# Attention scores: the second pass with 64 rows, two matmuls side by side in TensorE's array

## The chip, the cores and the metric

The kernel runs on one core of a Trainium2 chip. The core has a matrix engine (TensorE, in the profile PE for matmuls and PEld for its weight loads), three engines for everything else (VectorE, ScalarE and GpSimd: DVE, ACT, POOL) and a queue that issues most DMAs (SyncE, SP). The metric is the time of one execution in device microseconds (us); lower is better.

## The reference

One layer of a hybrid decoder, on 1024 tokens of width 1024 in float32. A projection feeds three mixers that run side by side; their outputs are normalised, mapped back by one output projection and added to the input; then comes an MLP. The mixer that matters here is the attention, with 8 query heads of 64 channels in 2 groups of 4 that share a key head. Its queries meet three sets of keys: compressed blocks, selected blocks, and a sliding window.

```python
s_c = jnp.einsum('bhgqd,bhnd->bhgqn', qb, kc) * scale        # compressed keys
...
s_s = jnp.einsum('bhgqd,bhqnld->bhgqnl', qb, k_sel) * scale  # selected blocks
...
s_w = jnp.einsum('bhgqd,bhkd->bhgqk', qb, kwb) * scale       # window of 512
...
o = gb[..., 0:1] * o_c + gb[..., 1:2] * o_s + gb[..., 2:3] * o_w
```

With 1024 tokens there are 16 blocks of 64 and 16 are selected, so the second branch sees all keys up to the query.

## The kernel before

The attention is worked through in sixteen units: one for each block of 128 queries (`i`) and each key head (`g`), four query heads (`h`) in a unit. A matmul here has 128 queries as its weights and runs the keys past them as columns; the scores of one head land in a tile of 1024 float32 in PSUM, two banks of 512.

The scores are computed with more accuracy than one pass of the fp32r format gives, by splitting both sides in a high and a low part. A channel dimension of 64 fills half of the array's 128 rows. The kernel therefore stacks the parts of the query: rows 0 to 63 of `qt` hold the high part and rows 64 to 127 the low part. The keys lie twice, once in each half of the rows: `kT[0]` holds their high part and `kT[1]` their low part. A matmul of `qt` with `kT[0]` gives high x high + low x high; a second one with `kT[1]` adds high x low + low x low.

`queries` makes `qt` for a unit: four transposes on TensorE, a copy of all 128 rows by ScalarE (L872), and a subtraction on rows 64 to 127 by VectorE (L873), which turns the copy there into the low part.

`scores` (L1034) serves one head whose keys are more than 512: it cuts the columns in two, one cut for each PSUM bank, and sends each cut through twice. `probs_few` (L1102) serves units with few keys, with two or four heads in one tile. Behind the scores `addmask` (L1042) and `mask` (L1108) add causal masks as matmuls of an identity in bf16. Then VectorE takes the maximum, ScalarE the exponential and GpSimd the scaling. `turn` (L1146) transposes the probabilities, and `values` (L1163, L1167) multiplies them with the values; the last piece of a unit's values, of the compressed branch, has 8 to 64 rows.

All these calls, with pieces of the output projection (`out_proj`, L896) as fillers, are sorted by due times that are written out by hand as fractions of a job, and are issued in that order; in the trace, pieces of neighbouring calls are at times interleaved on an engine. No due time is computed from an engine's cost.

Of the kernel before, what the change touches and what calls it, by code (L numbers as in the profile page):

```python
# [9 lines left out]
F32R = mybir.dt.float32r  # L10
BF16 = mybir.dt.bfloat16
I32 = mybir.dt.int32
AF = mybir.ActivationFunctionType
# [3 lines left out]
P = 128  # L17
# [5 lines left out]
DH = 64  # L23
# [13 lines left out]
def hymba_trunk(ctx: ExitStack, tc: tile.TileContext, ins: dict, out: bass.AP):  # L37
    nc = tc.nc
    act, dve, pool, pe = nc.scalar, nc.vector, nc.gpsimd, nc.tensor
# [11 lines left out]
    def f(ap):  # L51
        return ap.bitcast(F32)
# [19 lines left out]
    gq8 = cst.tile([P, 1], F32, name="gq8")  # L72
# [55 lines left out]
    def rpool(name):  # L128
        p_ = tc.tile_pool(name=name, bufs=1, side="right", reuse_waits="tile")
        right.append(p_)  # L130
        return p_.__enter__()
# [27 lines left out]
    with ExitStack() as pa:  # L159
# [554 lines left out]
        for s_, hf, b in proj_ch(C_KC, "kc"):  # L714
            o = hf * 512
# [34 lines left out]
        for qh in range(2):  # L750
            for t, b in proj_tok(C_Q + qh * 256, 256, f"q{qh}"):
# [4 lines left out]
                                  in_=sq.rearrange("p (a d) -> p a d", d=DH), axis=AX.X, op=ALU.add)  # L756
# [76 lines left out]
        kp2 = rpool("kp2")  # L833
        kwt = [[kp2.tile([P, S + 64], F32R, name=f"kwt{g}{j}") for j in range(2)] for g in range(2)]
        kst = [[kp2.tile([P, 64 + S], F32R, name=f"kst{g}{j}") for j in range(2)] for g in range(2)]
        qts = {}
# [23 lines left out]
        def queries(i, g, bank, qd):  # L860

            qd = qd.rearrange("p (h s d) -> p h s d", h=4, s=2)
            for s_ in range(2):
                pool.tensor_tensor(out=qd[:, :, s_, :],
                                   in0=qz[:, i, g * 256:(g + 1) * 256].rearrange("p (h d) -> p h d", d=DH),
                                   in1=rq[:, i * 8 + g * 4:i * 8 + g * 4 + 4][:, :, None].to_broadcast([P, 4, DH]), op=ALU.mult)
            yield
            b = bank(f"qT{i}{g}")
            for h in range(4):
                pe.transpose(b[:, h * P:(h + 1) * P], qd[:, h].rearrange("p s d -> p (s d)"), ident)  # L870
            qt = qts[i, g] = kp2.tile([P, 512], F32R, tag="qt", bufs=2, name=f"qt{i}{g}")
            act.activation(out=qt, in_=b, func=AF.Copy, scale=gq8)  # L872
            dve.scalar_tensor_tensor(out=qt[DH:P, :], in0=b[DH:P, :], scalar=gq8[DH:P, :], in1=f(qt[DH:P, :]),  # L873
                                     op0=ALU.mult, op1=ALU.subtract)

        lane(key_stack(1, 0, kdw, msbank))
        lane(queries(0, 0, msbank, spare[8]))
        for t in ks_:
            pass
# [119 lines left out]
    class Unit:  # L999
# [13 lines left out]
        def queries(self):  # L1013
            i, g = self.i, self.g
            if (i, g) not in qts:
                yield from queries(i, g, ring, spare[8])
            self.qt = qts.pop((i, g))
            self.nmx = uni.tile([P, 4, 3], F32, tag="nmx", bufs=2, name=f"nmx{i}{g}")
            self.sm = uni.tile([P, 4, 3], F32, tag="sm", bufs=2, name=f"sm{i}{g}")
            self.wt = uni.tile([P, 4, 3], F32, tag="wt", bufs=2, name=f"wt{i}{g}")  # L1020
            self.pc = uni.tile([P, 4, 64], F32, tag="pc", bufs=2, name=f"pc{i}{g}")

        def scores(self, h, kT, a, b_, name):

            n = b_ - a
            pt = psb.tile([P, 1024], F32, tag="s", bufs=2, name=name)
            if n <= 512:
                o, cuts = 0, [(0, n)]
            else:
                n0 = max(n - 512, min(512, n - 256))  # L1030
                o, cuts = 512 - n0, [(0, n0), (n0, n)]
            for (c0, c1) in cuts:
                for p_ in range(2):
                    pe.matmul(pt[:, o + c0:o + c1], self.qt[:, h * P:(h + 1) * P], kT[p_][:, a + c0:a + c1],  # L1034
                              start=p_ == 0, stop=False, skip_group_check=True)
            return pt, o

        @staticmethod
# [54 lines left out]
        def probs_few(self, br, h0):  # L1093

            i, g, m = self.i, self.g, self.few[br]
            kT, o, n = (kwt[g], 0, self.nw) if br == 2 else (kst[g], 64, self.nk)
            w, hs = 1024 // m, slice(h0, h0 + m)
            pt = psb.tile([P, 1024], F32, tag="s", bufs=2, name=f"sf{br}{i}{g}{h0}")
            by = pt.rearrange("p (h c) -> p h c", c=w)
            for j in range(m):  # L1100
                for p_ in range(2):
                    pe.matmul(pt[:, j * w:j * w + max(256, o + n)], self.qt[:, (h0 + j) * P:(h0 + j + 1) * P],  # L1102
                              kT[p_][:, 0:max(256, o + n)], start=p_ == 0 and j * w % 512 == 0, stop=False, skip_group_check=True)
            step_ = 512 // w

            def mask(c, mk, k):
                for j in range(0, m, step_):
                    pe.matmul(by[:, j:j + step_, c:c + k], identb, mk[:, None, :].to_broadcast([P, step_, k]),  # L1108
                              start=False, stop=True, skip_group_check=True)

            mask(o + n - P, m_causal, P)
            p_ = uni.tile([P, S], F32, tag="ps", bufs=PSB, name=f"pf{br}{i}{g}{h0}")
            parts = [(br, o, n, p_[:, 0:m * n].rearrange("p (h c) -> p h c", h=m))]
            if br == 1:
                mask(0 if i == 0 else 8 * i - 1, m_cmp[:, 1:9] if i == 0 else m_cmp, 8 if i == 0 else 9)
                parts.append((0, 0, self.ncm, self.pc[:, hs, :self.ncm]))
            for b_, c, k, dst in parts:
                dve.tensor_reduce(out=self.nmx[:, hs, b_], in_=by[:, 0:m, c:c + k], axis=AX.X, op=ALU.max, negate=True)
            for b_, c, k, dst in parts:
                for j in range(m):  # L1120
                    act.activation(out=dst[:, j, :], in_=by[:, j, c:c + k], func=AF.Exp, bias=self.nmx[:, h0 + j, b_:b_ + 1],
                                   accum_out=self.sm[:, h0 + j, b_:b_ + 1])
            for b_, c, k, dst in parts:
                wt = self.wt[:, hs, b_]
                gt = gates[:, i, :].rearrange("p (h b) -> p h b", b=3)[:, g * 4 + h0:g * 4 + h0 + m, b_]
                dve.reciprocal(wt, self.sm[:, hs, b_])
                dve.tensor_tensor(out=wt, in0=wt, in1=gt, op=ALU.mult)
                pool.tensor_tensor(out=dst, in0=dst, in1=wt[:, :, None].to_broadcast([P, m, k]), op=ALU.mult)
            for j in range(m):
                (self.pw if br == 2 else self.ps)[h0 + j] = parts[0][3][:, j, :]  # L1130
# [85 lines left out]
    for n, u in enumerate(units):  # L1216
# [5 lines left out]
        for part, br in ((0, 2), (1, 1)):  # L1222
# [3 lines left out]
            m = len(u.work[br])  # L1226
# [445 lines left out]
```

## Time and profile before

| | |
|---|---|
| median of three runs | 1255.13 us (1253.16 to 1256.38) |
| profiled execution, its own time | 1254.26 us |
| its span, first to last instruction | 1252.5 us |
| TensorE matmuls | 1205.0 us, 96% of the span, 6301 instructions |
| VectorE | 944.3 us, 75% |
| ScalarE | 675.8 us, 54% |
| GpSimd | 324.2 us, 26% |

A busy time is the union of an engine's instructions. Matmuls are pipelined, and the end of each is modelled, so that consecutive ones overlap on the page; the step from the start of one to the start of the next tells more than the duration. A form such as `64*128 64x512` means 64 rows and 128 columns of weights, and 512 columns that run past them.

### The profile page before, as it was taken

Reading aid. Unit: us, or ns where it says so; the run is one execution under the profiler, and the core shown is the slowest. Engines: PE = TensorE matmul, PEld = TensorE weight load, DVE = VectorE, ACT = ScalarE, POOL = GpSimd, SP = SyncE. Lnnn points to the kernel's source line nnn. Section 1 sums busy time; section 2 is a strip of 40 time slices with the busy share of each in tenths; the row PEclk is TensorE's granted clock in tenths of the full one; section 3 lists DMA queues with packets and bytes.
Section 4 is the critical chain, followed back from the end, with each engine's and each line's share of the span. In section 5 each row is a group of like instructions: output and inputs, shape, how many; then the busy total and the mean of one; then the engine's idle time right before and its main releaser. Section 6 shows DMA issues by size and latency. Waiting matters only on the chain.

```text
span 1252.5 us, 18215 instructions
## 1 busy us (share of the span) xinstructions
PE 1205.0 (96%) x6301; PEld 993.3 (79%) x6301; DVE 944.3 (75%) x1805; ACT 675.8 (54%) x1413; POOL 324.2 (26%) x347
## 2 busy tenths in 40 slices
PE   5999989979999999999799999999999999999998
PEld 5888878977777777777578888888878888888777
DVE  6899988658988989998867555555637897776684
ACT  6344367447677887776356545545544444444432
POOL 2357533335554456553760000000000000000000
PEclk9999999999999999999999999999999999999999
DMA  5322311212111200011424333333229933567640
GB/s 196 88 56 63 86 28 35 68 51 69 68 35 68 86 18 35 35 68 52 134 68 160 109 102 126 101 110 118 76 101 329 386 125 102 162 195 233 220 158 34
DMA packets 88584, 136.24 MB, mean 109 GB/s; under 512 B 8096, under 2 KB 42028, under 8 KB 88492
## 3 DMA queue, kind: packets, MB, share of 16 engines
q1 hardware_dynamic: 79276, 118.29, 29.2%
q10 hardware_dynamic: 9216, 16.78, 3.6%
q8 instruction: 50, 0.82, 0.3%
q14 instruction: 42, 0.34, 0.1%
HBM read 104.64 MB, written 29.36 MB: 107 GB/s over the span
## 4 chain that ended last, share of the span: by engine, by line
PE 81%; DVE 10%; ACT 3%; DMA 2%; POOL 2%; issue 1%; SPq 0%; ACTq 0%; DVEq 0%; POOLq 0%
PE y L1584 13%; PE z L1584 9%; PE t L1146 5%; PE rp L896 3%; PE op L896 3%; PE o L1163 3%; PE o L1167 3%; PE y L1387 2%; PE y L1389 2%; PE y L1388 2%; PE ss L1034 2%; DVE cv L515 2%; PE sw L1034 2%; PE kv L459 1%; PE kv L460 1%; PE kv L461 1%
## 5 line engine op out<-in xcount | busy, mean ns | idle before, releaser
L1149 ACT CAST ph<-t 128x512 fp32r<-128x512 f32 (+4 forms) x148 | 85.4, 585 | 44.6 <-PE t L1146 37.5
L1150 DVE TENSOR_TENSOR pl<-t,ph 128x512 fp32r<-128x512 f32 (+4 forms) x148 | 99.9, 683 | 6.1 <-ACT ph L1149 5.1
L1584 PE MATMUL y<-bl,ah 128*128 128x512 f32 x256 | 99.9, 390 | 1.8 <-DVE bl L1522 1.8
L1584 PE MATMUL y<-bh,al 128*128 128x512 f32 x256 | 99.6, 389 | 0.0
L1584 PE MATMUL y<-bh,ah 128*128 128x512 f32 x256 | 99.6, 389 | 0.0
L1304 ACT CAST whs<-s 128x512 fp32r<-128x512 f32 x64 | 39.9, 623 | 78.6 <-PE x L1388 32.1
L1584 PE MATMUL z<-bl,ah 128*128 128x512 f32 x192 | 75.0, 390 | 0.5 <-DVE bl L1522 0.5
L1584 PE MATMUL z<-bh,al 128*128 128x512 f32 x192 | 74.7, 389 | 0.0
L1584 PE MATMUL z<-bh,ah 128*128 128x512 f32 x192 | 74.7, 389 | 0.0
L1521 ACT CAST ah<-s 128x512 fp32r<-128x512 f32 x48 | 29.9, 623 | 75.7 <-PE y L1584 40.9
L214 POOL TENSOR_TENSOR wlo<-wst,whi 128x512 fp32r<-128x512 f32 (+1 forms) x36 | 52.6, 1474 | 61.8 <-ACT whi L213 61.5
L515 DVE SCALAR_TENSOR_TENSOR cv<-ypad,htap,cv 128x512 f32<-128x512 f32 x88 | 60.4, 752 | 0.4
L1305 DVE TENSOR_TENSOR wls<-s,whs 128x512 fp32r<-128x512 f32 x56 | 38.4, 685 | 26.6 <-ACT whs L1304 26.6
L1584 PEld LDWEIGHTS y<-bl,ah 128*128 128x128 f32 x256 | 48.1, 188 | 12.8 <-DVE bl L1522 2.8
L1584 PEld LDWEIGHTS y<-bh,ah 128*128 128x128 f32 x256 | 48.0, 188 | 10.0
L1584 PEld LDWEIGHTS y<-bh,al 128*128 128x128 f32 x256 | 48.0, 188 | 9.9
L1304 ACT CAST wha<-w 128x512 fp32r<-128x512 f32 x48 | 29.9, 622 | 39.1 <-PE y L1388 27.2
L1047 DVE TENSOR_REDUCE nmx<-ss 128x1 f32<-128x640 f32 (+8 forms) x72 | 43.5, 613 | 7.4 <-PE ss L1042 6.9
L1338 ACT ACTIVATE c<-c 128x512 f32<-128x512 f32 x48 | 30.4, 633 | 34.7 <-DVE c L1368 22.2
L1305 DVE TENSOR_TENSOR wla<-w,wha 128x512 fp32r<-128x512 f32 x42 | 28.9, 689 | 23.7 <-ACT wha L1304 23.6
L1521 ACT CAST ah<-x 128x512 fp32r<-128x512 f32 x32 | 19.9, 622 | 47.7 <-PE z L1584 34.2
L1522 DVE TENSOR_TENSOR al<-s,ah 128x512 fp32r<-128x512 f32 x48 | 33.2, 692 | 15.2 <-ACT ah L1521 14.8
(527 smaller groups left out, 3940.1 us busy)
## 6 DMA issues: line engine op xcount, KB each, us to landing
in<-in_mlp_w_dram SPq DMA_DIRECT2D x96, 256.0 KB
w<-in_mlp_w_dram SPq DMA_DIRECT2D x32, 512.0 KB
hid<-c ACTq DMA_DIRECT2D x48, 256.0 KB
in<-hid SPq DMA_DIRECT2D x48, 256.0 KB
wst<-in_w_in_dram SPq DMA_DIRECT2D x32, 256.0 KB
xr<-in_x_dram SPq DMA_DIRECT2D x8, 512.0 KB
x1p<-xr SPq DMA_DIRECT2D x8, 512.0 KB
x<-x1p SPq DMA_DIRECT2D x8, 512.0 KB
```

Of the source, the lines that this page charges most:

```text
L214: split[0] = pool.tensor_tensor(out=lo[:, :m], in0=st[:, :m], in1=f(hi[:, :m]), op=ALU.subtract).ins
L515: dve.scalar_tensor_tensor(out=acc[hf], in0=yp[:, o:o + 512], scalar=tap(k, ct), in1=acc[hf], op0=ALU.mult, op1=ALU.add)
L896: pe.matmul(b, a_[:, c * P:(c + 1) * P], w_, start=c == c0 and n == 0, stop=c == c1 - 1 and n == 2)
L1034: pe.matmul(pt[:, o + c0:o + c1], self.qt[:, h * P:(h + 1) * P], kT[p_][:, a + c0:a + c1], start=p_ == 0, stop=False, skip_group_check=True)
L1047: dve.tensor_reduce(out=nmx, in_=pt[:, c:c + n], axis=AX.X, op=ALU.max, negate=True)
L1146: pe.transpose(tb[:kn, h * P:(h + 1) * P], src(h), ident)
L1149: act.copy(ph[:kn], tb[:kn])
L1150: dve.tensor_tensor(out=pl[:kn], in0=tb[:kn], in1=f(ph[:kn]), op=ALU.subtract)
L1304: act.copy(k4(hi), v)
L1305: eng.tensor_tensor(out=k4(lo), in0=v, in1=f(k4(hi)), op=ALU.subtract)
L1521: act.copy(hi, v)
L1584: pe.matmul(banks2[BANK[m]][t], a_[:, ts], b_, start=q == 0 and n == 0 and m in FIRST, stop=q == NPAIR - 1 and n == 2, skip_group_check=True)
```

## The change

The second pass, with the low part of the keys, is done with the 64 rows of the query's high part alone; the product low x low is left out. `queries` makes a second tile `qx` that holds the high part in rows 64 to 127, beside `qt`, whose rows 0 to 63 hold it as before. ScalarE's one copy of 128 rows becomes two copies of 64 rows each. `scores` cuts its columns into halves, sends both through with `kT[0]` and full rows, and then issues two matmuls with `kT[1]`: the first cut on rows 0 to 63 with `qt`, the second on rows 64 to 127 with `qx`. They write different PSUM banks. `probs_few` does the same with pairs of heads. The number of matmuls is the same.

```diff
--- before.py
+++ after.py
@@ -868,9 +868,13 @@
             b = bank(f"qT{i}{g}")
             for h in range(4):
                 pe.transpose(b[:, h * P:(h + 1) * P], qd[:, h].rearrange("p s d -> p (s d)"), ident)
-            qt = qts[i, g] = kp2.tile([P, 512], F32R, tag="qt", bufs=2, name=f"qt{i}{g}")
-            act.activation(out=qt, in_=b, func=AF.Copy, scale=gq8)
-            dve.scalar_tensor_tensor(out=qt[DH:P, :], in0=b[DH:P, :], scalar=gq8[DH:P, :], in1=f(qt[DH:P, :]),
+            qt = kp2.tile([P, 512], F32R, tag="qt", bufs=2, name=f"qt{i}{g}")
+            qx = kp2.tile([P, 512], F32R, tag="qx", bufs=2, name=f"qx{i}{g}")
+            qts[i, g] = qt, qx
+
+            act.activation(out=qx[DH:P, :], in_=b[DH:P, :], func=AF.Copy, scale=gq8[DH:P, :])
+            act.activation(out=qt[0:DH, :], in_=b[0:DH, :], func=AF.Copy, scale=gq8[0:DH, :])
+            dve.scalar_tensor_tensor(out=qt[DH:P, :], in0=b[DH:P, :], scalar=gq8[DH:P, :], in1=f(qx[DH:P, :]),
                                      op0=ALU.mult, op1=ALU.subtract)
 
         lane(key_stack(1, 0, kdw, msbank))
@@ -1014,7 +1018,7 @@
             i, g = self.i, self.g
             if (i, g) not in qts:
                 yield from queries(i, g, ring, spare[8])
-            self.qt = qts.pop((i, g))
+            self.qt, self.qx = qts.pop((i, g))
             self.nmx = uni.tile([P, 4, 3], F32, tag="nmx", bufs=2, name=f"nmx{i}{g}")
             self.sm = uni.tile([P, 4, 3], F32, tag="sm", bufs=2, name=f"sm{i}{g}")
             self.wt = uni.tile([P, 4, 3], F32, tag="wt", bufs=2, name=f"wt{i}{g}")
@@ -1024,15 +1028,19 @@
 
             n = b_ - a
             pt = psb.tile([P, 1024], F32, tag="s", bufs=2, name=name)
+            hs = slice(h * P, (h + 1) * P)
             if n <= 512:
-                o, cuts = 0, [(0, n)]
-            else:
-                n0 = max(n - 512, min(512, n - 256))
-                o, cuts = 512 - n0, [(0, n0), (n0, n)]
+                o = 0
+                for p_ in range(2):
+                    pe.matmul(pt[:, 0:n], self.qt[:, hs], kT[p_][:, a:b_], start=p_ == 0, stop=False, skip_group_check=True)
+                return pt, o
+            n0 = max(n // 2, n - 512)
+            o, cuts = 512 - n0, [(0, n0), (n0, n)]
             for (c0, c1) in cuts:
-                for p_ in range(2):
-                    pe.matmul(pt[:, o + c0:o + c1], self.qt[:, h * P:(h + 1) * P], kT[p_][:, a + c0:a + c1],
-                              start=p_ == 0, stop=False, skip_group_check=True)
+                pe.matmul(pt[:, o + c0:o + c1], self.qt[:, hs], kT[0][:, a + c0:a + c1], start=True, stop=False, skip_group_check=True)
+
+            for (c0, c1), q_, rows in zip(cuts, (self.qt, self.qx), (slice(0, DH), slice(DH, P))):
+                pe.matmul(pt[:, o + c0:o + c1], q_[rows, hs], kT[1][rows, a + c0:a + c1], start=False, stop=False, skip_group_check=True)
             return pt, o
 
         @staticmethod
@@ -1097,10 +1105,15 @@
             w, hs = 1024 // m, slice(h0, h0 + m)
             pt = psb.tile([P, 1024], F32, tag="s", bufs=2, name=f"sf{br}{i}{g}{h0}")
             by = pt.rearrange("p (h c) -> p h c", c=w)
+            c1 = max(256, o + n)
             for j in range(m):
-                for p_ in range(2):
-                    pe.matmul(pt[:, j * w:j * w + max(256, o + n)], self.qt[:, (h0 + j) * P:(h0 + j + 1) * P],
-                              kT[p_][:, 0:max(256, o + n)], start=p_ == 0 and j * w % 512 == 0, stop=False, skip_group_check=True)
+                pe.matmul(pt[:, j * w:j * w + c1], self.qt[:, (h0 + j) * P:(h0 + j + 1) * P], kT[0][:, 0:c1],
+                          start=j * w % 512 == 0, stop=False, skip_group_check=True)
+
+            for j0 in range(m // 2):
+                for j, q_, rows in ((j0, self.qt, slice(0, DH)), (j0 + m // 2, self.qx, slice(DH, P))):
+                    pe.matmul(pt[:, j * w:j * w + c1], q_[rows, (h0 + j) * P:(h0 + j + 1) * P], kT[1][rows, 0:c1],
+                              start=False, stop=False, skip_group_check=True)
             step_ = 512 // w
 
             def mask(c, mk, k):
```

## Rows read from the trace of the kernel before

**Rows 1.** Stretches: us; busy (instructions) of PE, PEld, DVE, ACT, POOL; PEclk; DMA share; GB/s.
```profile
262.00:310.00 48.00, 39.52 (x261) 33.04 (x259) 36.15 (x79) 29.81 (x110) 20.17 (x24) 0.96 0.21 71
310.00:600.00 290.00, 287.69 (x1725) 224.31 (x1723) 258.00 (x581) 212.38 (x526) 145.09 (x181) 1.00 0.15 53
```

**Rows 2.** Chain that ended last, 310 to 600 us, shares by line.
```profile
by line: PE t L1146 20.3%; PE op L896 12.9%; PE o L1163 11.9%; PE rp L896 11.6%; PE o L1167 11.3%; PE ss L1034 9.7%; PE sw L1034 7.0%; PE sf L1102 3.4%; PE qT L870 1.7%; PE ss L1042 1.6%; PE sw L1042 1.6%; issue 1.2%; ACT ph L1149 1.0%; DVE
```

**Rows 3.** Waits, 262 to 310 us: engine, line, releaser; total, times, longest.
```profile
PE t L1146 <- DVE wt L1127: 4.9, 1, 4.9
```

**Rows 4.** Lines L1034, L1102: count, ns min/median/max, first and last start, forms.
```profile
L1034 PE MATMUL ss<-kst,qt x160: 276/369/501, 357.8 to 570.2; 128*128 128x512 f32 x64, 128*128 128x320 f32 x32, 128*128 128x448 f32 x32, 128*128 128x256 f32 x32
L1034 PE MATMUL sw<-kwt,qt x128: 277/312/471, 348.6 to 558.5; 128*128 128x256 f32 x64, 128*128 128x384 f32 x48, 128*128 128x448 f32 x16
...
L1102 PE MATMUL sf<-kwt,qt x64: 277/338/582, 270.0 to 462.4; 128*128 128x256 f32 x32, 128*128 128x384 f32 x16, 128*128 128x512 f32 x16
L1102 PE MATMUL sf<-kst,qt x48: 278/310/454, 271.1 to 345.4; 128*128 128x256 f32 x16, 128*128 128x320 f32 x16, 128*128 128x448 f32 x16
```

**Rows 5.** TensorE in order of time, two stretches: start, us, what, count.
```profile
500.59 0.75 PE L1034 MATMUL sw<-kwt,qt 128*128 128x384 f32 x4
501.18 0.23 PE L1042 MATMUL sw<-mwin,identb 128*128 128x128 bf16 x1
...
1100.12 0.39 PE L1584 MATMUL z<-bh,ah 128*128 128x512 f32 x1
...
1100.80 0.39 PE L1584 MATMUL y<-bh,ah 128*128 128x512 f32 x1
```

**Rows 6.** Lines L1163 and L1167: the matmuls on the compressed branch's values.
```profile
L1163 PE MATMUL o<-ph,vct x16: 489/497/502, 289.7 to 598.8; 8*128 8x512 f32 x2, 16*128 16x512 f32 x2, 24*128 24x512 f32 x2, 48*128 48x512 f32 x2
...
L1167 PE MATMUL o<-pl,vct x16: 383/394/448, 290.0 to 599.8; 8*64 8x512 f32 x2, 16*64 16x512 f32 x2, 24*64 24x512 f32 x2, 48*64 48x512 f32 x2
```

**Rows 7.** Around the 64-row matmuls, 598 to 600.6 us: TensorE, then one load.
```profile
598.24 0.40 PE L1167 MATMUL o<-pl,vst 128*64 128x512 f32 x1
598.47 0.40 PE L1163 MATMUL o<-ph,vst 128*128 128x512 f32 x1
598.80 0.50 PE L1163 MATMUL o<-ph,vct 64*128 64x512 f32 x1
599.22 0.44 PE L1167 MATMUL o<-pl,vst 128*64 128x512 f32 x1
599.50 0.40 PE L896 MATMUL op<-wo,ah 128*128 128x512 f32 x1
599.83 0.44 PE L1167 MATMUL o<-pl,vct 64*64 64x512 f32 x1
600.20 0.50 PE L896 MATMUL op<-wo,ah 128*128 128x512 f32 x1
...
598.79 0.18 PEld L1163 LDWEIGHTS o<-ph,vct 64*128 64x128 f32 x1 [0.37 <-issue]
```

**Rows 8.** Weight loads of two 16-row matmuls.
```profile
321.28 0.18 PEld L1163 LDWEIGHTS o<-ph,vct 16*128 16x128 f32 x1
321.39 0.13 PEld L1167 LDWEIGHTS o<-pl,vct 16*64 16x64 f32 x1
```

**Rows 9.** A mask between two 32-row matmuls, TensorE.
```profile
495.25 0.49 PE L1163 MATMUL o<-ph,vct 32*128 32x512 f32 x1
495.67 0.18 PE L1042 MATMUL ss<-mcmp,identb 128*128 128x9 bf16 x1
495.78 0.44 PE L1167 MATMUL o<-pl,vct 32*64 32x512 f32 x1
```

**Rows 10.** Query copies L872, L873; idle of TensorE ahead of L1102.
```profile
L872 ACT ACTIVATE qt<-qT,gq x16: 663/690/740, 258.5 to 539.9; 128x512 fp32r<-128x512 f32 x16
...
L873 DVE SCALAR_TENSOR_TENSOR qt<-qT,gq,qt x16: 756/757/760, 259.4 to 540.8; 64x512 fp32r<-64x512 f32 x16
...
  DVE qt L873: 4.5, 5
```

## The prediction

> **What bounds the kernel now.** I read the stretches first. From 262 to 600 us, the attention over the sixteen units, the stage from 310 on keeps TensorE busy for 287.7 of 290 us at the full granted clock (1.00, the 2.4 GHz level), while VectorE has 258.0, ScalarE 212.4 and GpSimd 145.1 [rows 1]. A busy TensorE may still be a badly modelled one, so the second view is the chain that ended last, from 310 to 600: eleven TensorE lines lead it with 93% together, and the score lines are among them (L1034 ss 9.7%, sw 7.0%, L1102 3.4%) [rows 2]. So here a TensorE microsecond is a microsecond of the end, nearly one for one. Before 310, 8.5 of 48 us are idle [rows 1], 4.9 of them one wait for the first unit's weights [rows 3]; that unit's scores lie ahead of this wait, so their time counts too. VectorE, next in line, has 32 us of room from 310 on.
>
> The third view is the list of score instructions. L1034 has 160 + 128 matmuls, four for a call: 72 calls. L1102 has 64 + 48, which are 6 calls with four heads (eight matmuls of 256) and 16 with two heads: 22 calls [rows 4]. Every one is 128x128 with full rows. Half of each sum is the second pass: 53,760 columns in L1034, 13,312 in the two-head calls, 6,144 in the four-head calls.
>
> **What a matmul costs.** The printed duration holds a tail that overlaps the next one; the step from start to start is what counts. At 512 columns four matmuls in a row start from 1100.12 to 1100.80, three steps of 0.227 us [rows 5]. The four score matmuls of 384, 384, 256, 256 columns from 500.59 to the mask at 501.18 take 0.59 [rows 5]. Two equations: 0.016 us + 0.41 ns a column. Weight loads do not appear in it: they run under the matmul ahead.
>
> **What the change removes.** With the two halves fully side by side, half of the second-pass columns and one of two starts go: L1034 26,880 columns x 0.41 ns + 72 x 0.016 = 12.2 us; two-head calls 6,656 columns and 16 starts = 3.0; four-head calls 3,072 columns and 12 starts = 1.4. Sum 16.6 us. The first pass has the same columns in other cuts (all at least 288 wide): nothing.
>
> **What it adds on TensorE.** The number of matmuls stays, but between the first pass and the mask stand matmuls with 64 rows. The trace has 64-row and smaller ones already: the values of the compressed branch, 16 on L1163 and 16 on L1167 [rows 6]. Around them the steps are longer. The clearest stretch is the last [rows 7], all of 512 columns, where 0.23 is normal:
> - 128 rows at 598.47 to 64 rows at 598.80: 0.33. The weight load of the 64-row one starts only at 598.79, so it waited until the array had finished: **0.10 to drain**.
> - 64 rows at 598.80 to 128 rows at 599.22: 0.42. It is 0.21 of columns, another 0.10 to drain, and 0.11 that the 64-row weight load takes in the open.
> - 599.50 to 599.83, into 64 rows once more: 0.33, the same 0.10.
> - 598.24 to 598.47, from 64 columns to 128 with all rows: 0.23, nothing. It is the change of rows that costs.
>
> A 32-row one behaves alike: 0.42 from 495.25 to 495.67 [rows 9]. So for each of the 94 calls:
> 1. Draining ahead of the pair: 0.10.
> 2. The first 64-row load in the open: 0.11 [rows 7].
> 3. The second load. No row shows weights for the upper 64 rows. The nearest: among small-row matmuls a load may run under a matmul, but two loads follow each other by 0.11 (321.28, 321.39) [rows 8]. If so, the second matmul starts 0.11 behind the first and the pair ends 0.11 late. Bounds: 0, if both loads run at once, to 0.11; I take 0.11.
> 4. Draining behind the pair: 0.10.
> 5. The mask's weights in the open. A nine-column mask just after a 32-row matmul steps 0.11 to the next, which changes rows again [rows 9]: 0.10 of it drains, so the bf16 load is about 0.02.
>
> Together 0.44 us a call, 41.4 for 94. In the four-head calls four loads follow each other, 0.44 from the first, and the last matmul ends 0.10 later than steps 2 and 3 allow: 6 x 0.1 = 0.6. Sum 42.0, net **42.0 - 16.6 = +25.4 us**. A call with 640 columns, say: second pass before 0.29, after 0.44 + 0.15 = 0.59.
>
> The Trainium skill ("TensorEngine Tiling (Array Packing)", Key Properties) says that a change of tiling mode drains the array and a change of tile alone does not. Rows 7 show the first half; no row here shows the second. By that rule nothing drains between the two matmuls of a pair, as my sum has it.
>
> **What it adds elsewhere.** The copy L872 (0.69 us, 16 times) becomes two copies of 64 partitions. No row shows a copy of 64 partitions; the subtraction L873 works on 64 and takes 0.757 [rows 10], so I take the full 0.69 for each half: at most 16 x 0.69 = 11 us more on ScalarE, which has 77 us of room from 310 on [rows 1]. VectorE waits only for the first of the two, and works 0.76 while ScalarE does the other, so the query is ready no later. TensorE waited 4.5 us in all for a query [rows 10]; what queues behind the new copy on ScalarE is the next cast of L1149, 0.69 later. TensorE grows slower than its suppliers, so I price this at 0; with the cover gone it would be 0.69 for a late query, 11 at the very most. The masks, VectorE's and GpSimd's instructions and the DMAs stay. Four KB more a partition for the second query tile lie in space whose earlier users, the projections, are ahead of the transposes on TensorE anyway: 0.
>
> **What is given back.** Waits of TensorE that other engines end get shorter when TensorE comes later: of the 8.5 + 2.3 us idle [rows 1] most is the 4.9 behind the first unit's own scores; I take 2 back (bounds 0 and 4). So 1254.26 + 25.4 - 2 = 1277.7. The profiled run lies 0.9 below the median 1255.13; I say **1277.5**.
>
> **Rivals.**
> - *Both loads at once* (step 3 is 0): 94 x 0.33 = 31.0, less 16.6 = +14.4, less 2: 1266.7. Against it, the 0.11 between two loads [rows 8]; for it, those were for the same rows. The skill ("TensorE: Matmul & The Clock Gate", Part 3) says that loads run beside matmuls when their row groups differ and that packed tiles start about 4 ns apart; if that holds with both loads still to do, this rival is the outcome. Chance 0.13.
> - *The halves do not overlap*: the second load then hides under the first matmul and the second pass keeps its columns; 94 x 0.33 = +31, less 2: 1283.3. No row shows two matmuls in the array at once. The gap to my forecast is small, because the late second load eats most of the overlap. Chance 0.15.
> - *Each matmul of a pair drains, too*: no overlap, and 0.21 more a pair (steps 1 and 2 again): 100 pairs x 0.21 = 21 on top of the last one: 1304. Chance 0.05.
> - *The rows change without a stop*, the one on the other side: the work side by side, 16.6 us gone, 1237.7 (VectorE's 258.0 of then 273 us would still fit). For it, the free change of columns [rows 7]; against it all the 32 small-row matmuls. It decides once entering and leaving cost less than 16.6 / 94 = 0.18 us a call, where I count 0.44. Chance 0.08.
> - *No change to be seen*: the call costs about what it saves, 0.14 to 0.24 with the 2 us given back; step 3 gone and the draining half as long would do it: 94 x 0.23 - 16.6 - 2 = +3, 1257. Chance 0.04.
>
> **How the numbers follow.** My forecast has 0.55. The two slower neighbours and the quick loads keep to one side, and with them 0.83 lies from 1264 (quick loads, 4 us given back: 1264.7) to 1289 (no overlap, nothing given back, and a few pairs torn apart by a transpose that TensorE runs in between, at some 0.3 each). Three runs of before lie within 0.26%, so 0.3%, 3.8 us, is what can be told from no change. Slower by more: 0.55 + 0.13 + 0.15 + 0.05 = 0.88; within: 0.04; faster: 0.08.
>
> **What would show it.** In the profile after, the weight load of the first 64-row matmul starts when the matmul ahead has ended, 0.10 late; the second load 0.11 behind it; the start of the pair's second matmul within 0.15 of the first, not a whole matmul later; the second pass with what surrounds it 0.59 us at 640 columns, in place of 0.29. The attention stage grows by some 23 us and all behind it moves as a block. VectorE's and ScalarE's idle time grows. The prediction is wrong if the 64-row load runs under the first pass, if a TensorE wait for the query tiles grows to some us, or if the granted clock leaves 1.00 in this stage.

## The result

The changed kernel takes 1274.58 us in the median of five runs (1271.64 to 1279.25), against 1255.13 before: a ratio of 1.0151, 95% interval 1.0137 to 1.0165. It is 19 us slower. 1277.5 was forecast, with a range of 1264 to 1289. Its profiled execution is the slowest of the five, 1279.25 us with a span of 1277.2. Of the runs below, one execution of switch_twice took 3171 us and one of copy_pool 5746 us; the ratios leave these two out, the medians count them.

### The profile page after: what moved, and what is told of

Same layout as the page of the kernel before. It is cut to its first block, busy times and chain, and to the rows that moved or that the text cites. A ratio compares the mean times of both kernels' runs of the same rounds, so it can differ in the third digit from the quotient of the medians.

```text
span 1277.2 us, 18230 instructions
## 1 busy us (share of the span) xinstructions
PE 1224.7 (96%) x6301; PEld 983.6 (77%) x6301; DVE 949.7 (74%) x1805; ACT 687.8 (54%) x1429; POOL 324.4 (25%) x347
## 4 chain that ended last, share of the span: by engine, by line
PE 80%; DVE 10%; ACT 4%; POOL 3%; DMA 2%; issue 1%; SPq 0%; ACTq 0%; POOLq 0%; DVEq 0%
PE y L1597 13%; PE z L1597 9%; PE t L1159 4%; PE rp L900 3%; PE op L900 3%; PE o L1176 2%; PE o L1180 2%; PE y L1400 2%; PE y L1402 2%; PE y L1401 2%; DVE cv L515 2%; PE kv L459 1%; PE kv L460 1%; PE kv L461 1%; PE y L1342 1%
## 5 line engine op out<-in xcount | busy, mean ns | idle before, releaser
L1163 DVE TENSOR_TENSOR pl<-t,ph 128x512 fp32r<-128x512 f32 (+4 forms) x148 | 99.6, 683 | 5.6 <-ACT ph L1162 4.3
L214 POOL TENSOR_TENSOR wlo<-wst,whi 128x512 fp32r<-128x512 f32 (+1 forms) x36 | 50.9, 1426 | 61.5 <-ACT whi L213 61.1
L1597 PEld LDWEIGHTS y<-bl,ah 128*128 128x128 f32 x256 | 48.3, 189 | 12.5 <-DVE bl L1535 2.3
L1055 DVE TENSOR_REDUCE nmx<-ss 128x1 f32<-128x768 f32 (+8 forms) x72 | 43.7, 617 | 11.0 <-PE ss L1050 10.5
```

What stands on the lines that cost most here:

```text
L214: split[0] = pool.tensor_tensor(out=lo[:, :m], in0=st[:, :m], in1=f(hi[:, :m]), op=ALU.subtract).ins
L1055: dve.tensor_reduce(out=nmx, in_=pt[:, c:c + n], axis=AX.X, op=ALU.max, negate=True)
L1163: dve.tensor_tensor(out=pl[:kn], in0=tb[:kn], in1=f(ph[:kn]), op=ALU.subtract)
L1597: pe.matmul(banks2[BANK[m]][t], a_[:, ts], b_, start=q == 0 and n == 0 and m in FIRST, stop=q == NPAIR - 1 and n == 2, skip_group_check=True)
```

## The profile after

The page's first part, and the granted clock in 40 slices of the span:

```profile
PE 1224.7 (96%) x6301; PEld 983.6 (77%) x6301; DVE 949.7 (74%) x1805; ACT 687.8 (54%) x1429; POOL 324.4 (25%) x347
...
PEclk9999989988999999999989999999999999999999
```

The number of matmuls is the same. ScalarE has 16 instructions and 12 us more.

Two stretches of the attention, with the columns of [rows 1]:

```profile
262.00:310.00 48.00, 39.17 (x243) 30.91 (x242) 34.64 (x75) 29.22 (x106) 19.35 (x24) 0.93 0.20 67
310.00:600.00 290.00, 283.40 (x1631) 197.70 (x1630) 246.70 (x535) 213.57 (x524) 144.27 (x179) 0.98 0.13 46
```

From 310 on TensorE is busy for 283.4 of 290 us, where it was 287.7 [rows 1]: it waits more than before. The granted clock is 0.98 in this stretch, where it was 1.00: for 10.2 us from 311 on it is at half, the 1.2 GHz level. The same 10.3 us in the profile after and in the one before:

```profile
311.00:321.30 10.30, 9.79 (x37) 6.96 (x35) 6.52 (x13) 6.53 (x22) 2.68 (x3) 0.51 0.17 53
311.00:321.30 10.30, 10.30 (x61) 8.36 (x59) 9.50 (x24) 6.81 (x23) 6.94 (x10) 1.00 0.00 1
```

That costs about half of the 10.2 us, 5 us (an estimate). The last score matmul starts at 593.3, where it was 570.2 [rows 4]; this is the line of the second pass, upper rows:

```profile
L1043 PE MATMUL ss<-kst,qx x40: 393/449/502, 370.1 to 593.3; 64*128 64x416 f32 x8, 64*128 64x352 f32 x8, 64*128 64x288 f32 x8, 64*128 64x480 f32 x8
```

The chain that ended last, 310 to 622 us:

```profile
by line: PE t L1159 17.8%; PE op L900 11.8%; PE rp L900 11.0%; PE o L1176 9.7%; PE o L1180 9.3%; PE ss L1040 4.4%; PE ss L1043 4.3%; PE sw L1040 3.5%; PE sw L1043 3.3%; PE sf L1115 2.3%; PE sf L1110 2.3%; PE ss L1050 2.3%; PE sw L1050 2.2%;
```

It is still TensorE's, and the second pass (L1043, L1115) has its own share in it, 10% with ss, sw and sf together.

One call of 640 columns in order of time, matmuls first and then weight loads:

```profile
520.64 0.46 PE L1040 MATMUL sw<-kwt,qt 128*128 128x320 f32 x2
521.02 0.41 PE L1043 MATMUL sw<-kwt,qt 64*128 64x320 f32 x1
521.03 0.41 PE L1043 MATMUL sw<-kwt,qx 64*128 64x320 f32 x1
521.37 0.23 PE L1050 MATMUL sw<-mwin,identb 128*128 128x128 bf16 x1
521.44 0.22 PE L1050 MATMUL sw<-mcausal,identb 128*128 128x128 bf16 x1
...
521.02 0.18 PEld L1043 LDWEIGHTS sw<-kwt,qt 64*128 64x128 f32 x1 [0.19 <-issue]
521.03 0.18 PEld L1043 LDWEIGHTS sw<-kwt,qx 64*128 64x128 f32 x1
521.37 0.11 PEld L1050 LDWEIGHTS <-identb 128*128 128x128 bf16 x2 [0.16 <-issue]
```

The two first passes start at 520.64, 0.15 apart, and the pair at 521.02: 0.09 after the second of them should have ended. The first 64-row load starts there too, with TensorE's loads idle for 0.19 before it. **The second load and the second matmul start within 0.01 us of the first**, and not 0.11 behind. From the pair to the mask it is 0.35 us: 0.11 for the loads, 0.13 for 320 columns, 0.10 to drain. The whole second pass takes 0.44, where 0.59 was forecast and it took 0.29 before. So each call is 0.15 longer; over 94 calls, 94 x 0.30 of entering and leaving less the 16.6 us saved are about 12 us. To check this I added up, over every score matmul of the trace, the time from its start to the start of TensorE's next matmul: 73.8 us before, 86.5 after. That is 12.7 of 19 us; some 1.5 of the 12.7 come from the clock (an estimate: 4.9 us of these steps lie at half clock, where it was 1.9, and half of the difference is lost). The rest had to be looked for.

## The experiments

All ratios are against the kernel before, run on the same chip.

| run | median us | ratio | 95% interval |
|---|---|---|---|
| low_rows | 1287.08 | 1.0250 | 1.0235 to 1.0265 |
| full_rows | 1265.78 | 1.0079 | 1.0064 to 1.0094 |
| switch_twice | 1314.58 | 1.0467 | 1.0449 to 1.0484 |
| two_heads | 1275.13 | 1.0160 | 1.0138 to 1.0183 |
| cuts_only | 1256.38 | 1.0000 | 0.9992 to 1.0009 |
| copies_only | 1264.24 | 1.0066 | 1.0049 to 1.0082 |
| copy_pool | 1272.36 | 1.0116 | 1.0098 to 1.0133 |
| after_again | 1276.99 | 1.0147 | 1.0127 to 1.0166 |
| copies_late | 1260.20 | 1.0030 | 1.0019 to 1.0042 |
| copy_late | 1268.63 | 1.0099 | 1.0086 to 1.0112 |
| two_heads_tight | 1270.37 | 1.0113 | 1.0098 to 1.0127 |
| no_copy | 1264.33 | 1.0070 | 1.0058 to 1.0083 |

**Do the two halves overlap? (low_rows)** The upper matmul of each pair moves to the lower rows. It computes the same values.

```diff
-            for (c0, c1), q_, rows in zip(cuts, (self.qt, self.qx), (slice(0, DH), slice(DH, P))):
+            for (c0, c1), q_, rows in zip(cuts, (self.qt, self.qt), (slice(0, DH), slice(0, DH))):
...
-                for j, q_, rows in ((j0, self.qt, slice(0, DH)), (j0 + m // 2, self.qx, slice(DH, P))):
+                for j, q_, rows in ((j0, self.qt, slice(0, DH)), (j0 + m // 2, self.qt, slice(0, DH))):
```

> Both second-pass matmuls of a pair use rows 0 to 63, so they cannot lie side by side; the number of changes of rows stays. If the two halves do overlap in the changed kernel, each pair here is longer by one matmul of half the columns: 12.2 + 3.0 + 1.4 = 16.6 us in all, so about 16 us over the changed kernel (1291). Rival, that the 3 ns between their starts is only how the profile shows them and they run one after the other: no change against the changed kernel (1275).

Measured 1287.1, 12.5 us over the changed kernel's median. TensorE in order of time, one call of 640 columns again:

```profile
530.00 0.53 PE L1040 MATMUL sw<-kwt,qt 128*128 128x320 f32 x2
530.46 0.56 PE L1043 MATMUL sw<-kwt,qt 64*128 64x320 f32 x2
530.95 0.23 PE L1050 MATMUL sw<-mwin,identb 128*128 128x128 bf16 x1
```

From the pair to the mask it is now 0.49 us, where the changed kernel has 0.35. The difference, 0.14, is one matmul of 320 columns (0.15 by the prediction's price). The overlap is real. All score steps together sum to 101.1 us, 14.6 over the changed kernel, where 16.6 was expected; some 1.4 of the missing 2.0 are the changed kernel's own half clock (2.1 us of these steps lie there in low_rows, against 4.9). 12.5 show in the time.

**Is it the changes of rows? (full_rows, switch_twice)** The first keeps all of the change but runs the second pass on all 128 rows. The second changes rows twice in each of the 72 calls of `scores`.

```diff
# full_rows
+            for (c0, c1), q_, rows in zip(cuts, (self.qt, self.qt), (slice(0, P), slice(0, P))):
...
+                for j, q_, rows in ((j0, self.qt, slice(0, P)), (j0 + m // 2, self.qt, slice(0, P))):
# switch_twice
-            for (c0, c1) in cuts:
-                pe.matmul(pt[:, o + c0:o + c1], self.qt[:, hs], kT[0][:, a + c0:a + c1], start=True, ...)
             for (c0, c1), q_, rows in zip(cuts, (self.qt, self.qx), (slice(0, DH), slice(DH, P))):
+                pe.matmul(pt[:, o + c0:o + c1], self.qt[:, hs], kT[0][:, a + c0:a + c1], start=True, ...)
                 pe.matmul(pt[:, o + c0:o + c1], q_[rows, hs], kT[1][rows, a + c0:a + c1], start=False, ...)
```

> The changed kernel with its new cuts, its second query tile and ScalarE's extra copies, but with the second pass on all 128 rows again, so TensorE never changes rows for the scores. If the changes of rows are the cause, this is the kernel before: 1255, within 2 us. Rival, that the copies, the tile or the order of work that comes with them cost the 5 to 6 us by which the time lies over what the score matmuls alone add: 1260.

> In the 72 calls of the longer rows the order is first pass of cut 0, second pass of cut 0, first pass of cut 1, second pass of cut 1, so TensorE enters and leaves the 64-row form twice a call. If each change of rows has its price (0.10 to drain, 0.11 for a 128-column load in the open), a call has 0.42 us more and loses its overlap (12.2 us in all): 72 x 0.42 + 12.2 = 42 us over the changed kernel, 1317. Rival, that the price belongs to a 64-row matmul whatever stands beside it: only the overlap is lost, 1287.

The doubled changes cost what their price says: 1314.6, 40 us over the changed kernel, where 42 was expected and the rival had 12. But full_rows missed its main expectation. Without any change of rows it is still 10 us slower than the kernel before. So the rows account for only about half of the loss, and the change has a second cost, which the prediction put at nothing.

**Which part is the second cost? (cuts_only, copies_only)** cuts_only is full_rows with `queries` and its one tile as before. copies_only is the kernel before with the new `queries`:

```diff
-            qt = qts[i, g] = kp2.tile([P, 512], F32R, tag="qt", bufs=2, name=f"qt{i}{g}")
-            act.activation(out=qt, in_=b, func=AF.Copy, scale=gq8)
+            qt = kp2.tile([P, 512], F32R, tag="qt", bufs=2, name=f"qt{i}{g}")
+            qx = kp2.tile([P, 512], F32R, tag="qx", bufs=2, name=f"qx{i}{g}")
+            qts[i, g] = qt, qx
+            act.activation(out=qx[DH:P, :], in_=b[DH:P, :], func=AF.Copy, scale=gq8[DH:P, :])
+            act.activation(out=qt[0:DH, :], in_=b[0:DH, :], func=AF.Copy, scale=gq8[0:DH, :])
...
```

> The kernel before with the new cuts and the new order (both first passes, then both second passes) alone: one query tile, one copy of 128 rows, all matmuls on 128 rows. If ScalarE's copies and the second query tile are what made the full-row version 10 us slower, this is the kernel before: 1255, within 2 us. Rival, that the cuts and the order cost it: 1265.

> The kernel before with the second query tile and ScalarE's two 64-row copies alone; the scores are as before. If the copies cost the 10 us: 1265. Rival, that the cuts and the order do: 1255. If each has a part, both lie between.

The cuts and the order of the passes cost nothing (1.0000). The copies cost 8.3 us by themselves (1.0066). In copies_only TensorE is busy for 281.8 of 290 us, where the kernel before has 287.7:

```profile
310.00:600.00 290.00, 281.83 (x1679) 218.52 (x1678) 253.50 (x559) 218.07 (x533) 144.76 (x180) 0.99 0.14 49
```

**Where the copies hurt.** The last unit's query after: transposes on TensorE, ScalarE, then VectorE.

```profile
560.75 0.49 PE L870 MATMUL qT<-ident,spare 128*128 128x128 f32 x3
...
561.50 0.68 ACT L875 ACTIVATE qx<-qT,gq 64x512 fp32r<-64x512 f32 x1
562.21 1.12 ACT L1056 ACTIVATE ps<-ss,nmx 128x1024 f32<-128x1024 f32 x1
...
563.31 0.67 ACT L876 ACTIVATE qt<-qT,gq 64x512 fp32r<-64x512 f32 x1
...
564.10 1.43 DVE L988 SCALAR_TENSOR_TENSOR yf<-x,rm,gmn 128x512 f32<-128x512 f32 x2
...
565.69 0.76 DVE L877 SCALAR_TENSOR_TENSOR qt<-qT,gq,qx 64x512 fp32r<-64x512 f32 x1
```

And the same query before:

```profile
539.13 0.63 PE L870 MATMUL qT<-ident,spare 128*128 128x128 f32 x4
...
539.90 0.67 ACT L872 ACTIVATE qt<-qT,gq 128x512 fp32r<-128x512 f32 x1
...
540.83 0.76 DVE L873 SCALAR_TENSOR_TENSOR qt<-qT,gq,qt 64x512 fp32r<-64x512 f32 x1
```

Before, one copy follows the transposes, and VectorE ends its subtraction at 541.59. After, ScalarE does the first copy at 561.50, then an exponential of 1.1 us, then the second copy until 563.98; VectorE begins only at 565.69, since other work of its own (L988) stands ahead. The transposes end at 539.76 before and at 561.24 after (start and duration of their rows), so the way to the end of the subtraction has grown from 1.8 to 5.2 us. In the two units where VectorE stood idle ahead of the subtraction, it waited for the second copy:

```profile
L877 DVE SCALAR_TENSOR_TENSOR qt<-qT,gq,qx x16: 756/757/758, 261.5 to 565.7; 64x512 fp32r<-64x512 f32 x16
...
  ACT qt L876: 1.0, 2
```

In all 16 units the subtraction starts after the end of the second copy, by 0.03 to 1.7 us, though it reads only the first. That both write the tile `qt`, in different rows, is the likely reason; it was not tested apart. Added up over 16 units, it is 41.8 us from the end of the last transpose to the end of the subtraction before, and 63.1 after.

How TensorE pays for it can be read where the copies stand alone. Waits of its matmuls, 310 to 600 us, all of copies_only and then those for an exponential before:

```profile
PE ss L1046 <- ACT ps L1052: 1.6, 3, 0.7
PE sf L1106 <- ACT pf L1125: 1.3, 1, 1.3
PE t L1150 <- DVE qt L877: 1.2, 2, 0.7
PE sw L1038 <- ACT pw L1052: 1.1, 1, 1.1
PE sw L1038 <- ACT pc L1052: 1.0, 2, 0.8
PE rp L900 <- DVE qt L877: 0.9, 1, 0.9
PE sw L1038 <- DVE qt L877: 0.5, 1, 0.5
```

```profile
PE ss L1042 <- ACT ps L1048: 0.8, 2, 0.6
PE sf L1102 <- ACT pc L1048: 0.5, 2, 0.2
```

The query itself is waited for 2.6 us, where there was no such wait from 310 on; waits put down to exponentials grow from 1.3 to 5.0 us.

**Two other places for the copy. (copy_pool, copies_late, copy_late)** In copy_pool ScalarE's one copy of 128 rows goes into the second tile, and GpSimd copies rows 0 to 63 of it into the first. In copies_late (scores as before) and copy_late (scores as changed) the query is made as before and ScalarE's extra copy comes last.

```diff
# copy_pool
+            act.activation(out=qx, in_=b, func=AF.Copy, scale=gq8)
+            pool.tensor_copy(qt[0:DH, :], f(qx[0:DH, :]))
...
# copies_late, copy_late
+            act.activation(out=qt, in_=b, func=AF.Copy, scale=gq8)
+            dve.scalar_tensor_tensor(out=qt[DH:P, :], in0=b[DH:P, :], scalar=gq8[DH:P, :], in1=f(qt[DH:P, :]),
+                                     op0=ALU.mult, op1=ALU.subtract)
+            act.activation(out=qx[DH:P, :], in_=b[DH:P, :], func=AF.Copy, scale=gq8[DH:P, :])
```

> The changed kernel with one copy of 128 rows by ScalarE, as before, into the second tile, and GpSimd copying rows 0 to 63 of it into the first. ScalarE has no more work than before and frees the transposes' bank as early. If the copies cost 10 us there, 1265, still slower than before by the changes of rows. Rival, that they cost nothing or that GpSimd's copy makes the query late instead: 1275 or more.

> The kernel before (scores on 128 rows throughout) with the query made as before, one copy of 128 rows and then VectorE's subtraction, and the second tile's copy of 64 rows issued behind them. ScalarE has the same 11 us of extra copies as in copies_only (8.3 us slower than before). If the loss comes from the subtraction, which there starts only after the second copy, the query is as early as before and the time is 1255 to 1257. Rival, that ScalarE's time itself costs it: 1264 again.

> The changed kernel with the same order of copies: the 128-row copy, the subtraction, then the second tile's copy. If a late query costs 8 us there, what is left is the changes of rows: 12.6 us of steps over before, 1266 to 1268. Rival, ScalarE's time: 1275.

copies_late takes 1260.2, between its expectation and its rival: 3.8 us over before, where copies_only has 8.3. Its sum from transpose to subtraction is back at 43.1 us, and TensorE is busy for 285.1 of 290:

```profile
310.00:600.00 290.00, 285.14 (x1716) 221.48 (x1715) 255.18 (x571) 222.79 (x547) 146.78 (x183) 1.00 0.15 51
```

So somewhat more than half of the copies' cost was the late query. The other 3.8 us stay with ScalarE's extra copies even when the query is early; whether through their 11 us of ScalarE time, through the transposes' bank, which the last copy still reads as late as in copies_only (61.1 us after the transposes, added up, against 62.7), or through the other order in which the instructions of all engines then stand was not told apart. copy_late falls to 1268.6, about as expected. copy_pool, at 1272.4, gets back less than half of the 10 us that it was expected to. Its trace shows one reason: the subtraction is as early as before (42.6 us), but GpSimd's copy is late, and until the whole of `qt` is written it is 53.3 us, midway between 41.8 and 63.1.

**The same kernel once more (after_again).** 

> The changed kernel unchanged, for a profile with a granted clock nearer to the others' (its profiled run had 0.983 where four others had 0.989 to 0.992). If the clock's dips explain why that profile lies 5 us over the median, the span here is about 1270 to 1273 at 0.99, with the same steps around the pairs.

Ratio 1.0147, as before. Its profiled run again lay high (1277.7, span 1275.7, clock 0.987), and the same 10.2 us at half the clock stand at 310 us in it. So the first profile was no oddity. The clocks of all ten executions answer the question that it was run for: the four with a mean clock of 0.991 or 0.992 took 1271.6 to 1272.6 us, the six with 0.983 to 0.990 took 1274.6 to 1279.3. The kernel before, run beside the second five, took 1255.4 to 1256.5 at 0.992. So at equal clock the change costs about 16 us, and the rest of the 19 goes with the clock. Why it falls at 311 was not tested; in the profiles of cuts_only, full_rows, copies_late, copy_late and no_copy it stays at 1.00 from 310 to 600.

**The changes of rows alone (no_copy).** The query as before, and the upper matmul of a pair on rows 64 to 127 of `qt`, so low x low stands for high x low in half of the columns.

```diff
-            for (c0, c1), q_, rows in zip(cuts, (self.qt, self.qx), (slice(0, DH), slice(DH, P))):
+            for (c0, c1), q_, rows in zip(cuts, (self.qt, self.qt), (slice(0, DH), slice(DH, P))):
```

> The changes of rows alone: the query is made as in the kernel before, with one copy and no second tile, and the upper matmul of each pair takes rows 64 to 127 of that query, which hold its low part (this changes the product of half the columns: low x low in the place of high x low). If the two parts of the loss add up, the time is the kernel before plus what the changed kernel has over the full-row version, 9 us: 1264 to 1266. Rival, that the steps of the score matmuls count in full once the copies are away: 12.6 us, 1269.

1264.33, 1.0070: 8.8 us over before. The changed kernel has 0.70% over full_rows and copy_late 0.69% over copies_late: three separations of the same part agree. The score steps sum to 84.2 us here, 10.4 over before, so 1.6 of them are given back, within the interval (7.3 to 10.4 us of time). TensorE is busy through the stage, as before:

```profile
310.00:600.00 290.00, 288.10 (x1682) 203.69 (x1680) 252.07 (x559) 209.37 (x520) 144.21 (x181) 1.00 0.14 50
```

**Half as many changes of rows (two_heads, two_heads_tight).** Two heads at a time: both first passes, both pairs, then the masks. The second run also fixes that order for TensorE and takes the copies of copy_late.

```diff
+            for h in heads:
+                for (c0, c1) in cuts:
+                    x_ = pe.matmul(pts[h][:, o + c0:o + c1], self.qt[:, h * P:(h + 1) * P], kT[0][:, a + c0:a + c1], ...)
+            for h in heads:
+                for (c0, c1), q_, rows in zip(cuts, (self.qt, self.qx), (slice(0, DH), slice(DH, P))):
+                    with tc.issue_after(x_.ins):   # two_heads_tight alone
+                        x_ = pe.matmul(pts[h][:, o + c0:o + c1], q_[rows, h * P:(h + 1) * P], kT[1][rows, a + c0:a + c1], ...)
```

> The 72 calls of the longer rows are taken two heads at a time: both first passes, then both pairs, then the masks, so 36 changes into 64 rows and 36 out of them go. By the price of 0.31 a call that is 11 us less than the changed kernel, 1263. Rival, that the two score tiles in PSUM, both now held until both heads are reduced, make TensorE wait for them: the 11 us are eaten or more, 1275 and above.

> Two heads at a time as in two_heads, with the copies as in copy_late, and with an order given for TensorE so that both heads' pairs stand together: in two_heads 86 stretches of 64-row matmuls were left of 97, here 62 are. By 0.31 a stretch that is 35 x 0.31 = 11 us less than copy_late: 1256, about the kernel before. Rival, that holding both score tiles until both heads are reduced makes TensorE wait for PSUM: not under copy_late, 1267 or more.

two_heads tells nothing: in its trace the 64-row matmuls still stand in 86 stretches, of 97, since TensorE's order had put most pairs apart again. In two_heads_tight there are 62. TensorE, one call of two heads:

```profile
399.85 0.46 PE L1035 MATMUL sw<-kwt,qt 128*128 128x320 f32 x2
400.24 0.41 PE L1039 MATMUL sw<-kwt,qt 64*128 64x320 f32 x1
400.24 0.41 PE L1039 MATMUL sw<-kwt,qx 64*128 64x320 f32 x1
400.49 0.31 PE L1039 MATMUL sw<-kwt,qt 64*128 64x320 f32 x1
400.49 0.30 PE L1039 MATMUL sw<-kwt,qx 64*128 64x320 f32 x1
400.73 0.23 PE L1047 MATMUL sw<-mwin,identb 128*128 128x128 bf16 x1
```

Two pairs share one entry: 0.25 and 0.24 us for a pair, against 0.35 for one that stands alone with its drain. The score steps sum to 75.9 us, 10 less than in copy_late, about as expected (11). But the time is 1270.4, no better than copy_late's 1268.6. TensorE's busy time in the stage shows where it went, first copy_late, then two_heads_tight:

```profile
310.00:600.00 290.00, 286.24 (x1668) 200.91 (x1666) 250.87 (x559) 217.39 (x533) 145.26 (x182) 1.00 0.14 48
```

```profile
310.00:600.00 290.00, 279.48 (x1657) 198.23 (x1656) 249.75 (x559) 214.46 (x531) 144.97 (x182) 1.00 0.14 48
```

It is busy 6.8 us less: it waits. Its waits for exponentials, which free the PSUM tiles of the scores, grow from 2.2 to 6.0 us in this stretch; the longest in copy_late and the three longest in two_heads_tight:

```profile
PE sw L1040 <- ACT pc L1056: 1.1, 1, 1.1
```

```profile
PE ss L1047 <- ACT ps L1053: 3.0, 5, 1.4
PE sw L1047 <- ACT pw L1053: 1.2, 2, 0.9
PE sw L1035 <- ACT pc L1053: 1.1, 1, 1.1
```

The time is the rival's, 1267 or more, and these waits, 3.8 of the 6.8 us, are what it named. This run also fixes TensorE's order, and what the order costs by itself was not tried. No version tried here beats the kernel before.

## Why the prediction came out right

The direction holds, and so does the mechanism on TensorE: entering and leaving the 64-row form costs more than the overlap saves. That the total came within 3 us is luck: two terms were 13 us too high together, another was 8 us too low, and the clock was not in the sum.

- *TensorE bounds the stage*: held. In no_copy 10.4 us of steps became 8.8 us of time.
- *16.6 us saved*: held for a call (0.14 for 320 columns in low_rows); over all calls the steps give 14.6, the time 12.5.
- *Steps 1, 2 and 4, draining, load, draining*: 0.09, 0.11 and 0.10 measured for 0.10, 0.11, 0.10. switch_twice confirms them, 40 us for 42. *Step 5*, 0.02 for the mask's load, does not show: 0.35 is accounted for without it. That is 1.9 us for 94 calls.
- *Step 3, the second load 0.11 behind the first*: wrong; it costs nothing. It was mis-sized by 10.3 us for 94 calls and 0.6 for the four-head ones. The row that I took for nearest, two loads 0.11 apart [rows 8], was for the same rows. The rival of both loads at once was right in this: 1266.7, and no_copy has 1264.3. What the Trainium skill says of different row groups ("TensorE: Matmul & The Clock Gate", Part 3) and of tiles of one mode, between which nothing drains ("TensorEngine Tiling (Array Packing)", Key Properties), the trace bears out: loads and matmuls of a pair start within 0.01 us.
- *The copies at 0*: the step that failed. "VectorE waits only for the first of the two" is not so in any of 16 units: the query is ready 21 us later, added up over them, and the copies cost 8.3 us, within the 11 that the prediction named as the most. My argument was that TensorE becomes slower than its suppliers. But in copies_only its idle time from 310 to 600 grows from 2.3 to 8.2 us, in waits for the query and for the exponentials.
- *2 us given back*: 1.6 in no_copy, not clear of noise.
- *The clock at 1.00*: not so. Of the three signs of being wrong this one came, with 0.98 from 310 to 600, and the sum has no term for it. A second came in part: the waits of TensorE's matmuls for the query grow from 1.6 to 3.8 us (the 4.5 of [rows 10] adds 2.9 of its weight loads' waits). The 64-row load did not run under the first pass.
- *The last step of the sum*: 1277.7 was on the scale of the profiled run; the median lies 0.9 above it, so the sum meant 1278.5 there.

With the two errors put right the sum is 10.4 - 1.6 + 8.3 = 17 us, close to the 16 that the change costs at equal clock. The two parts measured apart, 0.70% and 0.66%, make 1.36%; the changed kernel has 1.51% and, in the second set of runs, 1.47% (1.27 to 1.66). The difference, 1 to 2 us, fits the executions at a lower clock.

## What to carry to other kernels

Packing two 64-row matmuls beside full-row ones has an entry price: here 0.30 us for each stretch of them, against at most 512 x 0.41 ns + 0.016 = 0.23 us that one pair in it can save. So a single pair per stretch could not pay at any width in this kernel. Two pairs of 512 columns in one stretch would save more than the 0.30, by these numbers; no run here shows a gain from it, and in two_heads_tight waits of TensorE took back what the steps had gained. And an edit that adds a copy to the making of an operand is priced by when the operand is then ready, with all that stands between its parts on the engines, and not only by whether the engine has idle time: an experiment that keeps the copies and undoes the rest shows it in one run.

## What had not been expected of the hardware

The weight loads of the two 64-row halves, of 128 columns each, start within 0.01 us of each other and cost the time of one (0.11 us); the matmuls run in full overlap (0.35 us from pair to mask, 0.49 when both use the same rows). Leaving 64 rows for a bf16 mask costs about 0.10 us, as much as the drain into them (0.09), so nothing is left for the load of the mask's weights.
